# Block places given back in turn, a last output block done token tile by token tile, and W11 loaded once, in a one-core transformer block on Trainium2

## The chip, the core and the metric

The kernel runs on one core of a Trainium2 chip. The core has five engines with an instruction stream each: TensorE (PE; its weight loads are listed apart as PEld), VectorE (DVE), ScalarE (ACT), GpSimd (POOL) and SyncE (SP). Sixteen DMA engines move the data; loads are issued by SP, by ACT or, for loads that add onto what is there, by POOL. The metric is the time of one execution in microseconds (us): three runs of the kernel before gave 2258.97, 2261.0 and 2263.16, median 2261.0.

## What is computed

One block of a transformer in fp32, for one sequence of S = 512 tokens of width D = 2048, with a feed-forward width FF = 5632. The part that matters here is what follows the mixing of tokens:

```
sh_a, sc_a, g_a, sh_f, sc_f, g_f = split(silu(c) @ ada_w + ada_b, 6)      # "ada": six vectors of 2048
h = modulate(rms_norm(x, norm_mix), sh_a, sc_a);  proj = h @ w_in          # then convolutions and sparse attention
x = x + g_a * (concat(y_conv, y_attn) @ w_out)                             # out projection
h = modulate(rms_norm(x, norm_ffn), sh_f, sc_f)
x = x + g_f * ((silu(h @ ffn_w1) * (h @ ffn_w3)) @ ffn_w2)                 # FFN up, FFN down
```

## The kernel before

Each fp32 operand of a matmul is split in two parts, `hi` (rounded) and `lo` (the rest), and a product is lo·hi + hi·lo + hi·hi, three matmuls. A weight block is loaded by DMA, ACT casts it to `whi` (`w_hi`, L948) and DVE subtracts to get `wlo` (L953, L1262). The order in which each engine does its work is set by a scheduler from the program and its priorities; a tile's place is taken again only after the last reader of its former tile. SP issues its loads strictly in order: one that waits for a place holds all behind it.

The stages, in times of the profiled execution: input projection, compression and part of the ada vectors up to about 310 us; convolutions, attention and more ada up to 680; the out projection from 715 to 904; FFN up from 916 to 1791; FFN down from 1792 to 2257, and a short tail.

**Ada parts.** The FFN's shift, scale and gate are made by `ffn_parts`, a generator that is woven beside other work: one part is 16 loads of 256 KB and 16 instructions of DVE (L185). Parts 0 to 2 run beside `token_blocks` (up to 310 us), 3 to 9 beside the convolutions and the attention, the last two beside the last output block.

**Out projection to FFN up.** The output is made in four blocks of 512 columns (`token_block`, L98 to L100, three matmuls of 128x512 per token tile and 128 rows of weights). In a block, pairs of weight rows are the outer loop and the four token tiles the inner one, so the four tiles end together. Then, per tile, DVE multiplies by the gate and adds (L891, L892), and ACT takes the sum of squares (L893). After the fourth block follow the factor 1/rms of each token (L905 to L907, spread over partitions by the matmul L908), the transposes of the last block (`x2_turned(3)`, L871), the modulation of h (`modulated`, L985 on DVE and L986 on ACT, 128x512 for each of 16 k's), and `h_parts` (L976, L977), which splits h into the blocks `hC` that the products read.

**FFN up** is one level of Strassen: 44 units of 128 columns, for each of which seven products are formed from the blocks `hC[p]`, p = 1, 5, 6, 3, 7, 2, 4 (`product`, L960 and L962). The first two units (`PLAIN`) use four plain products from `hC[1..4]` while `h_sums` makes the rest. All `hC` lie in one pool, closed after the last unit.

**FFN down** is Strassen over four groups b of 5, 6, 6 and 5 units j, with seven products p per group in the order 1, 5, 6, 3, 7, 2, 4 (1, 2, 5, 6, 3, 7, 4 in group 0): 154 units of 12 matmuls 128x512 (L1282). The weights of a unit are four blocks W11, W12, W21, W22 of 512 KB, loaded by `w_load` a number of units ahead (`AHEAD`):

- p = 1: W11, into the ring `raw`
- p = 5: W11 again into a place of `t` (6 places), then W12 added onto it (L1237, POOL)
- p = 6: W22 into one of the 6 places `w`; DVE adds it to t (L1256). p = 3 uses W22 itself, so its place is free only after p3's split
- p = 7: W12 into a place of `w`, then W22 added (L1237, POOL)
- p = 2: W21 into a place of `w`; p = 4: W21 added onto t (L1251)

`a_parts` makes the other operand, `ghi`, `glo` and `e`, from gated rows `k0`, `k1` that `k_load` brings. `evict` adds finished products into y (L1301, L1303). `w_split` runs two units ahead of the matmuls.

Of the kernel before, what the change touches and what calls it, by code (L numbers as in the profile page):

```python
# [69 lines left out]
def block_kernel(ctx: ExitStack, tc: tile.TileContext, a: dict, out: bass.AP):  # L70
# [576 lines left out]
    early = ffn_parts(wring, 512, range(3))  # L647
    weave(beside(token_blocks(), early, 3.2), before_attention(), 1.5)
# [185 lines left out]
    later = ffn_parts(wring, 512, range(3, 10))  # L834
    weave(beside(convs(), later, 1.9), attention_steps(), 0.68)
# [19 lines left out]
    gd = [dram.tile([P, S], F32, name=f"gd{f}") for f in range(FF // P)]  # L855
    hst = ExitStack()
# [4 lines left out]
    xp = pool("x2", 2, stack=gst)  # L861
    tp = pool("tmp", 2, stack=gst)
    aring = pool("aring2", 3, stack=gst)
# [15 lines left out]
    for n in range(4):  # L879
        if n < 3:  # L880
            x_load(n + 1)
        ga = tp.tile([P, 512], F32, tag="ga", name="ga")
        ada_bcast(aux, ga, acc_g[-1])
        pst = [main() for _ in range(NT)]
        side = ada(aring, 1024, 2 * D + (n + 1) * 512, 512, acc_g, bias=True) if n < 3 else \
            ffn_parts(aring, 1024, (10, 11))
        weave(token_block(w_out, n * 512, yT, every[8:] + every[:8], pst), side, 1 if n < 3 else 2.5)
        for i, ps in enumerate(pst):
            t = tp.tile([P, 512], F32, tag="t", name="t")
            x2 = x2s[n][:, i, :]  # L890
            nc.vector.tensor_mul(t, ps, ga)  # L891
            nc.vector.tensor_add(x2, x2, t)  # L892
            nc.scalar.activation(t, x2, AF.Square, accum_out=ss2[:, i, n:n + 1])  # L893
        for i in range(0, NT, 2):
# [6 lines left out]
    rb = aux()  # L901
    for i in range(NT):
        dg = tp.tile([P, P], F32, tag="dg", name="dg")
        r2 = tp.tile([P, 1], F32, tag="r2", name="r2")
        nc.vector.reduce_sum(r2, ss2[:, i, :], axis=AX)  # L905
        rsqrt(r2, r2, D)
        nc.vector.tensor_scalar(dg, ident, r2, None, op0=ALU.mult)  # L907
        nc.tensor.matmul(rb[:, i * P:(i + 1) * P], ones, dg, start=True, stop=True)  # L908
# [11 lines left out]
    HS, HK = S // 2, KC // 2  # L920
    ust = ExitStack()
    dp = pool("up", 2)
    t2p = pool("t2", 1)
    hcp = pool("hC", 1, stack=ust)
    hC = {p: hcp.tile([P, HK, S], F32R, name=f"hC{p}") for p in (1, 5, 6, 3, 7, 2, 4)}
# [30 lines left out]
    def product(ps, wt, p, first, last):  # L956

        ks = [slice(k * P, (k + 1) * P) for k in range(HK)]
        for k in range(HK):
            nc.tensor.matmul(ps, wt[0][:, ks[k]], hC[p][:, k, :], start=first and k == 0, stop=False, skip_group_check=True)  # L960
        for k in range(HK):
            nc.tensor.matmul(ps[:, HS:], wt[1][:, ks[k]], hC[p][:, k, 0:HS], start=False, stop=last and k == HK - 1,  # L962
                             skip_group_check=True)
# [16 lines left out]

    def modulated(j, c, n, lower):

        for k in range(j * HK + c, j * HK + c + n):
            h = x2T[:, k, :]
            nc.vector.scalar_tensor_tensor(h, h, gsc[:, 1, k:k + 1], rb, op0=ALU.mult, op1=ALU.mult)  # L985
            nc.scalar.activation(h, h, AF.Identity, bias=shf[:, 1, k:k + 1])  # L986
        h_parts(1 + j, A[0, j][:, c:c + n, :], c, n)
        h_parts(lower, A[1, j][:, c:c + n, :], c, n)

    def h_sums(step):  # L990
# [4 lines left out]
        elif step == 1:  # L995
            nc.vector.tensor_sub(A[1, 1], A[1, 1], A[1, 0])
            h_parts(5, A[1, 1], 0, HK)
        elif step == 2:
# [15 lines left out]
    def plain_steps(u):  # L1014
# [3 lines left out]
        def make(q, w, j):  # L1018
# [3 lines left out]
            def mm(s):  # L1022
                if j == 0:
                    o[w] = [(main, aux)[w]() for _ in range(2)]
                for i, p in ((0, 1 + j), (1, (3, 4)[j])):
                    product(o[w][i], (s["hi"], s["lo"]), p, j == 0, j == 1)
# [15 lines left out]
        return [make(q, w, j) for q, w, j in ((11, 0, 0), (21, 0, 1), (12, 1, 0), (22, 1, 1))]  # L1042
# [67 lines left out]

    def k_load(b, half):
        n = GS[b]
        t = kraw[b, half] = krp.tile([P, GM, S], F32, tag=f"k{half}", name=f"k{half}")
        for j in range(n):
            nc.gpsimd.dma_start(t[:, j, :], gd[START[b] + half * n + j])
# [45 lines left out]
    modulated(0, 0, 2, 3)  # L1161
    modulated(0, 2, 2, 3)
    modulated(0, 4, 4, 3)
    for n, s in enumerate(order):
# [7 lines left out]
        if n < 4 * PLAIN:  # L1172
            h_sums(n)
        if n == len(order) - 5:
            zst.close()
            krp = pool("kraw", 1, side="right")
            for half in range(2):
                k_load(0, half)
        s["mm"](s)
        if n + 1 < len(order):  # L1180
            s["post"](s)
    ust.close()
# [5 lines left out]
    gpp = pool("gparts", 3)  # L1188
    tz = pool("tz", GM)
    wz = pool("wz", 6)  # L1190
    ep = pool("e", 1)
    yp = pool("y2", 3)
    yq = pool("y3", 1, side="right")
    y2 = [(yq if t == 3 else yp).tile([P, D], F32, tag="y", name="y") for t in range(NT)]
# [7 lines left out]
    def a_parts_(b, p):  # L1202
# [18 lines left out]
        hi = gpp.tile([P, GM, HS], F32R, tag="ghi", name="ghi")  # L1221
        lo = gpp.tile([P, GM, HS], F32R, tag="glo", name="glo")
# [4 lines left out]
    def w_load(b, p, j):  # L1227
# [5 lines left out]
        def get(pl, tag, one, plus=None):  # L1233
            t = pl.tile([P, HN], F32, tag=tag, name=tag)
            nc.sync.dma_start(t, one)
            if plus is not None:
                nc.gpsimd.dma_start(t, plus, accum_op=ALU.add)  # L1237
            return t

        if p == 1:  # L1240
            W[b, 11, j] = get(ring[0], "raw", block(0, 0))
        elif p == 5:
            W[b, "t", j] = get(tz, "t", block(0, 0), block(0, 1))
        elif p == 6:
            W[b, 22, j] = get(wz, "w", block(1, 1))
        elif p == 7:
            W[b, "t3", j] = get(wz, "w", block(0, 1), block(1, 1))
        elif p == 2:
            W[b, 21, j] = get(wz, "w", block(1, 0))
# [8 lines left out]
    def w_split(b, p, j):  # L1258
        t = W[b, {1: 11, 5: "t", 6: "t", 3: 22, 7: "t3", 2: 21, 4: "t"}[p], j]
# [76 lines left out]
    AHEAD = {1: 4, 5: 9, 6: 6, 7: 7, 2: 6, 4: 10}  # L1336

    def loads(n):
        for m in range(n + 13, n + 3, -1):
            if 0 <= m < len(units):  # L1340
                b, p, j = units[m]
                if (12 if (b, p) == (0, 5) else AHEAD.get(p)) == m - n:
                    w_load(b, p, j)

    for n in range(-13, 0):
        loads(n)
    for m in range(2):
        w_split(*units[m])
# [5 lines left out]
    for n, (b, p, j) in enumerate(units):  # L1354
# [16 lines left out]
        if n + 2 < len(units):  # L1371
            w_split(*units[n + 2])
# [35 lines left out]
```

## Time and profile before

| | before |
|---|---|
| median of three runs | 2261.0 us |
| profiled execution, its own time | 2263.49 us |
| its span (first to last instruction) | 2261.7 us |
| PE busy | 2182.5 us, 96% |
| DVE busy | 1725.9 us, 76% |
| ACT busy | 996.1 us, 44% |
| moved by DMA | 446.72 MB |

The time of a run is 1.8 us more than the span of its trace. Busy times are sums over instructions; matmuls are pipelined, so one shows 0.39 us while the next starts 0.23 us after it.

### The profile page before, as it was taken

The page shows a single profiled execution, that of the slowest core. Times are in us where ns is not written, and L with a number is a line of the kernel's source. Part 1 is how long each engine was busy: PE and PEld are TensorE (multiplying, and loading weights), DVE is VectorE, ACT ScalarE, POOL GpSimd, SP SyncE. Part 2 cuts the span into 40 slices and gives each one's busy share as a digit, 9 for nine tenths or more (in the row PEclk, how much of TensorE's full clock was granted, in tenths as well). Part 3 has the DMA queues.
Part 4 walks back from the last instruction along what each step waited for, and adds up shares of the span by engine and source line. Part 5 has one row for each costly group of instructions (what it writes and reads, how often), then busy time and mean ns, then how long its engine had stood idle before and what let it go on. Part 6 is the DMA issues. An engine that isn't in the chain of part 4 may idle for free.

```text
span 2261.7 us, 30554 instructions
## 1 busy us (share of the span) xinstructions
PE 2182.5 (96%) x11377; PEld 1812.0 (80%) x11377; DVE 1725.9 (76%) x2523; ACT 996.1 (44%) x1558; POOL 222.4 (10%) x267
## 2 busy tenths in 40 slices
PE   6999999999999999899999999999999998999998
PEld 5788778778777787788888888888888876777786
DVE  6878877877769755977878777887878776778697
ACT  5335235554444222744444444444444454444442
POOL 5310000000000000010000000000000121211111
PEclk9999999999999999999999999999999999999999
DMA  9965766544446865397776767677775699786966
GB/s 319 363 219 178 260 198 189 165 143 137 135 138 223 296 233 160 104 224 174 180 183 165 184 170 179 165 177 172 182 182 135 208 292 264 180 265 176 265 155 161
DMA packets 441096, 446.72 MB, mean 198 GB/s; under 512 B 18232, under 2 KB 345116, under 8 KB 440308
## 3 DMA queue, kind: packets, MB, share of 16 engines
q1 hardware_dynamic: 371764, 330.40, 46.7%
q0 software_dynamic: 69040, 114.12, 23.6%
q8 instruction: 89, 1.46, 0.3%
q14 instruction: 59, 0.48, 0.1%
q10 hardware_dynamic: 144, 0.26, 0.0%
HBM read 424.78 MB, written 19.93 MB: 197 GB/s over the span
## 4 chain that ended last, share of the span: by engine, by line
PE 73%; DMA 12%; DVE 11%; issue 2%; ACT 1%; POOL 0%; SPq 0%; DVEq 0%; ACTq 0%; POOLq 0%
PE main L960 14%; PE aux L960 10%; PE main L962 7%; PE main L98 6%; PE main L100 6%; PE main L99 6%; PE aux L1282 5%; PE aux L962 5%; DMA araw<-in_ada_w 5%; PE main L1282 5%; DMA w<-in_ffn_w 5%; DVE acc L185 2%; DVE wlo L1262 2%; PE aux L98 1%; DMA raw<-in_ffn_w 1%
## 5 line engine op out<-in xcount | busy, mean ns | idle before, releaser
L948 ACT CAST whi<-raw 128x1024 fp32r<-128x1024 f32 x282 | 295.3, 1047 | 351.5 <-PE main L960 114.0
L953 DVE TENSOR_TENSOR wlo<-raw,whi 128x1024 fp32r<-128x1024 f32 x260 | 315.4, 1218 | 81.2 <-ACT whi L948 80.8
L960 PE MATMUL main<-hC,whi 128*128 128x512 f32 x1408 | 356.7, 395 | 5.2 <-DVE hC L977 3.7
L960 PEld LDWEIGHTS main<-hC,whi 128*128 128x128 f32 x1408 | 255.1, 190 | 51.9 <-DVE hC L977 4.3
L960 PE MATMUL aux<-hC,whi 128*128 128x512 f32 x1072 | 270.1, 393 | 0.0
L185 DVE SCALAR_TENSOR_TENSOR acc<-araw,cT,acc 128x512 f32<-128x512 f32 x248 | 185.6, 748 | 73.2 <-DMA araw<-in_ada_w 60.2
L960 PEld LDWEIGHTS aux<-hC,whi 128*128 128x128 f32 x1072 | 193.7, 190 | 34.9
L962 PEld LDWEIGHTS main<-hC,wlo 128*128 128x128 f32 x1408 | 192.1, 190 | 13.8
L962 PE MATMUL main<-hC,wlo 128*128 128x256 f32 x1408 | 196.3, 282 | 0.0
L98 PE MATMUL main<-alo,whi 128*128 128x512 f32 x448 | 182.8, 408 | 1.4 <-DVE alo L347 1.4
L948 ACT CAST whi<-t 128x1024 fp32r<-128x1024 f32 x108 | 113.5, 1052 | 152.7 <-PE aux L1282 42.1
L99 PE MATMUL main<-ahi,wlo 128*128 128x512 f32 x448 | 176.6, 394 | 0.0
L100 PE MATMUL main<-ahi,whi 128*128 128x512 f32 x448 | 176.5, 395 | 0.0
L92 ACT CAST whi<-raw 128x1024 fp32r<-128x1024 f32 (+2 forms) x84 | 79.5, 949 | 207.0 <-PE main L100 138.6
L962 PEld LDWEIGHTS aux<-hC,wlo 128*128 128x128 f32 x1072 | 146.3, 190 | 12.4 <-DVE wlo L953 1.9
L98 PE MATMUL main<-wlo,ahi 128*128 128x512 f32 x384 | 152.9, 398 | 0.0
L99 PE MATMUL main<-whi,alo 128*128 128x512 f32 x384 | 151.8, 395 | 0.0
L962 PE MATMUL aux<-hC,wlo 128*128 128x256 f32 x1072 | 149.9, 282 | 1.5 <-DVE wlo L953 1.5
L100 PE MATMUL main<-whi,ahi 128*128 128x512 f32 x384 | 151.1, 394 | 0.0
L1262 DVE TENSOR_TENSOR wlo<-w,whi 128x1024 fp32r<-128x1024 f32 x66 | 79.9, 1222 | 81.3 <-ACT whi L948 81.2
L1282 PE MATMUL aux<-wlo,ghi 128*128 128x512 f32 x308 | 123.1, 400 | 16.2 <-DVE wlo L1262 16.2
L1049 DVE TENSOR_TENSOR raw<-raw 128x1024 f32<-128x1024 f32 x84 | 102.3, 1218 | 47.1 <-DMA raw<-in_ffn_w 47.0
(317 smaller groups left out, 4069.5 us busy)
## 6 DMA issues: line engine op xcount, KB each, us to landing
raw<-in_ffn_w SPq DMA_DIRECT2D x219, 512.0 KB, 4.9
araw<-in_ada_w SPq DMA_DIRECT2D x176, 256.0 KB, 3.0
w<-in_ffn_w SPq DMA_DIRECT2D x66, 512.0 KB, 8.0
t<-in_ffn_w POOLq DMA_DIRECT2D x65, 512.0 KB, 8.5
araw<-in_ada_w POOLq DMA_DIRECT2D x56, 512.0 KB, 14.4
raw<-in_w_in SPq DMA_DIRECT2D x128, 192.0 KB, 2.7
t<-in_ffn_w SPq DMA_DIRECT2D x43, 512.0 KB, 5.7
araw<-in_ada_w SPq DMA_DIRECT2D x40, 512.0 KB, 5.4
```

The source lines that it names most:

```text
L92: nc.scalar.copy(hi[:, :m], raw[:, :m])
L98: nc.tensor.matmul(ps, lhs[0], rhs[1], start=first, stop=False)
L99: nc.tensor.matmul(ps, lhs[1], rhs[0], start=False, stop=False)
L100: nc.tensor.matmul(ps, lhs[0], rhs[0], start=False, stop=last)
L185: nc.vector.scalar_tensor_tensor(acc, w, s, acc, op0=ALU.mult, op1=ALU.add)
L948: nc.scalar.copy(hi, t)
L953: nc.vector.tensor_sub(lo, t, hi.bitcast(F32))
L960: nc.tensor.matmul(ps, wt[0][:, ks[k]], hC[p][:, k, :], start=first and k == 0, stop=False, skip_group_check=True)
L962: nc.tensor.matmul(ps[:, HS:], wt[1][:, ks[k]], hC[p][:, k, 0:HS], start=False, stop=last and k == HK - 1, skip_group_check=True)
L1049: nc.vector.tensor_add(to, x, y)
L1262: W["last"] = nc.vector.tensor_sub(lo, t, hi.bitcast(F32)).ins
L1282: nc.tensor.matmul(ps[2 * t + c], x_[:, j, tok], w[:, cs], start=m == 0 and j == 0 and p in (1, 5, 2), stop=m == 2 and j == GS[b] - 1 and ...
```

## The change

Five things are done; the numbers in the code are those of the diff.

1. **Ada.** One of the early parts of `ffn_parts` is done in the later stage; both weaving rates follow.
2. **Last output block.** For the last four k's of block n = 3 both weight pairs are loaded, and the twelve matmuls of each token tile are done together, tile after tile; `normed(i)` then makes the tile's sum, squares and factor while the next tile's matmuls run.
3. **h by token groups.** The first half of K is modulated in halves of 256 tokens (`modulated_half`), and the products of unit 0 go chunk by chunk, with both weights.
4. **Places of hC.** Each block has a pool of its own and is given back after the last product that reads it; the places of the down phase (`kraw`, `tz`, `ghi`, `e`, `glo`, `wz`) take their room one by one.
5. **Weights of the down phase.** W11 is loaded once, into t, and split there for p1; W12 is added onto it right after that split. W22, W12 and W21 take ten places in turn, four of the ring `raw` and six `w`.

```diff
-    def token_block(w, c0, lhs, order, pst):
+    def token_block(w, c0, lhs, order, pst, each=None):
         for j in range(0, KC, 2):
+            if each and j == KC - 4:
+                wss = [load_split(ring, rows(w, order[jj], 2, c0, 512), 2, 512) for jj in (j, j + 2)]
+                for i in range(NT):
+                    tok = slice(i * P, (i + 1) * P)
+                    for k in range(4):
+                        mm3(pst[i], [h[:, tok] for h in lhs[order[j + k // 2 * 2] + k % 2]],
+                            [t[:, k % 2, :] for t in wss[k // 2]], False, k == 3)
+                    each(i)
+                    yield
+                return
...
-    early = ffn_parts(wring, 512, range(3))
-    weave(beside(token_blocks(), early, 3.2), before_attention(), 1.5)
+    early = ffn_parts(wring, 512, range(2))
+    weave(beside(token_blocks(), early, 3.5), before_attention(), 1.5)
...
-    later = ffn_parts(wring, 512, range(3, 10))
-    weave(beside(convs(), later, 1.9), attention_steps(), 0.68)
+    later = ffn_parts(wring, 512, range(2, 10))
+    weave(beside(convs(), later, 2.15), attention_steps(), 0.68)
...
+        def normed(i):
+            through(i)
+            if i % 2 == 0:
+                diag[i // 2] = accp.tile([P, S], F32, tag="acc", name="dg")
+            dg = diag[i // 2][:, i % 2 * P:(i % 2 + 1) * P]
+            r2 = tp.tile([P, 1], F32, tag="r2", name="r2")
+            nc.vector.reduce_sum(r2, ss2[:, i, :], axis=AX)
+            rsqrt(r2, r2, D)
+            nc.vector.tensor_scalar(dg, ident, r2, None, op0=ALU.mult)
+            if i == 1:
+                factor(0)
...
+            rb, diag = aux(), {}
+            weave(token_block(w_out, n * 512, yT, every[8:] + every[:8], pst, normed), side, 3.0)
...
+    def modulated_half(i, c, n, lower):
+        for k in range(c, c + n):
+            h = A[i, 0][:, k, :]
+            nc.vector.scalar_tensor_tensor(h, h, gsc[:, 1, k:k + 1], rb[:, i * HS:(i + 1) * HS], op0=ALU.mult,
+                                           op1=ALU.mult)
+            nc.scalar.activation(h, h, AF.Identity, bias=shf[:, 1, k:k + 1])
+        h_parts(lower if i else 1, A[i, 0][:, c:c + n, :], c, n)
...
+                if u == 0 and j == 0:
+                    for i in range(2 * w):
+                        if i:
+                            factor(1)
+                            for c in range(0, HK, 2):
+                                modulated_half(1, c, 2, 3)
+                        for k in range(HK):
+                            for v in range(2):
+                                product(o[v][i], (o["s", v]["hi"], o["s", v]["lo"]), (1, 3)[i], True, False, [k])
+                    return
...
+    def given_back(p):
+        hcst[p].close()
+        right = lambda *args: pool(*args, side="right")
+        if p == 1:
+            later["k"], later["t"] = right("kraw", 1), right("tz", GM)
+            for half in range(2):
+                k_load(0, half)
+        elif p in (5, 6, 3, 7):
+            name, n = {5: ("ghi", 3), 6: ("e", 1), 3: ("glo", 3), 7: ("wz", 6)}[p]
+            later[name] = right(name, n)
...
+        def place():
+            W["n"] = W.get("n", -1) + 1
+            pl, tag = (ring[0], "raw") if W["n"] % 10 < 4 else (wz, "w")
+            return pl.tile([P, HN], F32, tag=tag, name=tag)
...
         if p == 1:
-            W[b, 11, j] = get(ring[0], "raw", block(0, 0))
+            W[b, "t", j] = get(tz.tile([P, HN], F32, tag="t", name="t"), block(0, 0))
         elif p == 5:
-            W[b, "t", j] = get(tz, "t", block(0, 0), block(0, 1))
+            nc.gpsimd.dma_start(W[b, "t", j], block(0, 1), accum_op=ALU.add)
         elif p == 6:
-            W[b, 22, j] = get(wz, "w", block(1, 1))
+            W[b, 22, j] = get(place(), block(1, 1))
         elif p == 7:
-            W[b, "t3", j] = get(wz, "w", block(0, 1), block(1, 1))
+            t = W[b, "t3", j] = get(place(), block(0, 1))
+            nc.gpsimd.dma_start(t, block(1, 1), accum_op=ALU.add)
...
-    AHEAD = {1: 4, 5: 9, 6: 6, 7: 7, 2: 6, 4: 10}
+    AHEAD = {1: 5, 6: 9, 7: 12, 2: 9, 4: 15}
```

What the scheduler makes of it is seen in the order of instructions. TensorE at the end of the last output block, before (L908 spreads the factors, L871 are the transposes, L960 the first products of FFN up):

```order
L100 MATMUL main<-whi,ahi 128x512
L408 MATMUL aux<-acc,const 1x512
L908 MATMUL aux<-dg,const 128x128 x2
L871 MATMUL aux<-const,x_7437 128x128 x5
L908 MATMUL aux<-dg,const 128x128
L871 MATMUL aux<-const,x_7437 128x128
L908 MATMUL aux<-dg,const 128x128
L871 MATMUL aux<-const,x_7437 128x128 x10
L960 MATMUL main<-hC_8175,whi 128x512 x2
```

The same place now, from the second factor matmul inside the block (L915; the first stands ten rows further up) on; L890 are the transposes, L994 and L996 the products:

```order
L915 MATMUL aux<-dg,const 128x128
L100 MATMUL main<-whi,ahi 128x512
...
L99 MATMUL main<-whi,alo 128x512
L100 MATMUL main<-whi,ahi 128x512
L890 MATMUL aux<-const,x_7441 128x128 x12
L994 MATMUL main<-hC_6767,whi 128x512
L996 MATMUL main<-hC_6767,wlo 128x256
L994 MATMUL main<-hC_6767,whi 128x512
L996 MATMUL main<-hC_6767,wlo 128x256
L890 MATMUL aux<-const,x_7441 128x128 x4
```

The factors of tiles 0 and 1 have moved into the block, and the first products stand right behind twelve transposes; those of the second token half (L915 x2) follow seven rows below.

SyncE's loads in the down phase, before, from the end of group 0 on (raw is W11 for p1, t is W11 for p5, w is W22, W12 and W21):

```order
L1235 DMA w<-in_ffn_w 128x1024 x10
L1235 DMA t<-in_ffn_w 128x1024 x5
L1235 DMA raw<-in_ffn_w 128x1024 x6
L1235 DMA w<-in_ffn_w 128x1024 x18
L1235 DMA t<-in_ffn_w 128x1024 x6
L1235 DMA raw<-in_ffn_w 128x1024 x6
```

And now, from the first loads of group 1 to the W11 of group 2 (t is the one load of W11; raw and w are the ten places in turn):

```order
L1303 DMA w<-in_ffn_w 128x1024 x6
L1303 DMA raw<-in_ffn_w 128x1024 x4
L1303 DMA w<-in_ffn_w 128x1024
L1303 DMA t<-in_ffn_w 128x1024 x5
L1303 DMA w<-in_ffn_w 128x1024 x5
L1303 DMA raw<-in_ffn_w 128x1024 x4
L1303 DMA w<-in_ffn_w 128x1024 x6
L1303 DMA raw<-in_ffn_w 128x1024 x3
L1303 DMA t<-in_ffn_w 128x1024 x6
```

Of the 18 loads into places of a group, the first ten now stand ahead of the last five loads of its W11, and no W11 is loaded a second time.

GpSimd's adding loads of group 1, before (L1237 is W12 for p5 and W22 for p7, L1251 is W21 for p4, L1115 brings k):

```order
L1237 DMA t<-in_ffn_w 128x1024 x5
L1251 DMA t<-in_ffn_w 128x1024 x3
...
L1251 DMA t<-in_ffn_w 128x1024 x3
L1237 DMA w<-in_ffn_w 128x1024 x6
L1115 DMA k_17458<-gd_6748 128x512
```

And now (L1309 is W12 for p5, L1314 W22 for p7, L1318 W21 for p4):

```order
L1314 DMA raw<-in_ffn_w 128x1024 x3
L1314 DMA w<-in_ffn_w 128x1024
L1309 DMA t<-in_ffn_w 128x1024 x6
L1318 DMA t<-in_ffn_w 128x1024 x3
...
L1318 DMA t<-in_ffn_w 128x1024 x3
L1314 DMA w<-in_ffn_w 128x1024 x2
```

Four of the six sums for p7 are now issued ahead of all six for p5, where all six stood behind those for p4.

## Rows read from the trace of the kernel before

**Rows 1.** The page, first part: busy time, share of the span, instructions.

```profile
PE 2182.5 (96%) x11377; PEld 1812.0 (80%) x11377; DVE 1725.9 (76%) x2523; ACT 996.1 (44%) x1558; POOL 222.4 (10%) x267
```

**Rows 2.** List of waits, TensorE: releaser, us in total, times, longest us.

```profile
PE aux L1282 <- DVE wlo L1262: 16.2, 12, 3.7
PE main L1282 <- DVE wlo L1262: 14.7, 12, 4.7
```

**Rows 3.** Windows, line L1282 alone, of six products: span, busy (x), PEclk, DMA share, GB/s.

```profile
1807.00:1826.80 19.80, 15.69 (x61) 12.15 (x60) 0.91 1.04 322
1867.70:1891.70 24.00, 16.54 (x61) 12.49 (x61) 0.86 0.88 271
1969.40:1995.60 26.20, 20.88 (x86) 15.33 (x85) 1.00 1.05 309
...
2094.80:2120.70 25.90, 20.82 (x86) 15.28 (x85) 1.00 1.03 302
2208.70:2229.50 20.80, 15.84 (x62) 12.38 (x61) 0.92 0.96 240
...
2028.30:2046.10 17.80, 16.92 (x74) 13.37 (x73) 1.00 1.03 299
```

**Rows 4.** Chain that ended last, 1940 to 2030: start, us, what.

```profile
1966.58 11.44 DMA w<-in_ffn_w
...
1978.58 11.75 DMA w<-in_ffn_w
...
1995.82 16.32 PE main L1282 x72
```

**Rows 5.** Timeline of SyncE's queue, 1940 to 1996: start, us, loads.

```profile
1953.02 42.94 SPq L1235 DMA_DIRECT2D w<-in_ffn_w  x14
```

**Rows 6.** DMA of 1790 to 2230: queues (packets, MB, share), issues (median us to landing).

```profile
q0 software_dynamic: 12512, 44.57, 48.4%
q1 hardware_dynamic: 15557, 56.65, 35.0%
...
w<-in_ffn_w SPq DMA_DIRECT2D x66, 512.0 KB, 8.0
...
w<-in_ffn_w POOLq DMA_DIRECT2D x22, 512.0 KB, 11.0
```

**Rows 7.** Timeline of TensorE where FFN down begins.

```profile
1792.42 0.96 PE L1282 MATMUL main<-wlo,ghi 128*128 128x512 f32 x3 [1.65 <-ACT ghi L1223]
1793.95 0.50 PE L1282 MATMUL main<-whi,glo 128*128 128x512 f32 x1 [0.57 <-DVE glo L1224]
```

**Rows 8.** Timelines of TensorE and VectorE between out projection and FFN up.

```profile
904.06 0.39 PE L100 MATMUL main<-whi,ahi 128*128 128x512 f32 x1
...
916.54 2.08 PE L960 MATMUL main<-hC,whi 128*128 128x512 f32 x4 [3.75 <-DVE hC L977]
...
910.95 4.04 DVE L985 SCALAR_TENSOR_TENSOR x2T<-x2T,gsc,aux 128x512 f32<-128x512 f32 x6 [1.02 <-PE aux L908]
```

**Rows 9.** Groups by form of VectorE, 900 to 970, and a window of all engines.

```profile
L891 DVE TENSOR_TENSOR t<-main,ga 128x512 f32<-128x512 f32 x4 | 2.6, 687 | 0.2 <-ACT t L893 0.2
...
L971 DVE TENSOR_TENSOR d<-main,d 128x256 f32<-128x256 f32 x5 | 2.0, 417 | 0.1
...
917.00:943.60 26.60, 26.60 (x136) 22.70 (x136) 25.36 (x27) 23.70 (x30) 0.00 (x0) 0.89 0.14 41
```

**Rows 10.** Ada: its group on VectorE, and windows (PE, PEld, DVE, ACT, POOL busy).

```profile
L185 DVE SCALAR_TENSOR_TENSOR acc<-araw,cT,acc 128x512 f32<-128x512 f32 x248 | 185.6, 748 | 73.2 <-DMA araw<-in_ada_w 60.2
...
296.00:310.00 14.00, 11.04 (x42) 7.85 (x41) 8.28 (x21) 4.58 (x7) 0.00 (x0) 0.88 0.79 229
310.00:680.00 370.00, 366.60 (x1861) 294.21 (x1860) 280.02 (x591) 181.18 (x417) 2.10 (x4) 1.00 0.51 151
```

**Rows 11.** Timeline of VectorE in the last group's product 7.

```profile
2211.68 1.23 DVE L1262 TENSOR_TENSOR wlo<-w,whi 128x1024 fp32r<-128x1024 f32 x1 [3.74 <-ACT whi L948]
...
2218.42 2.35 DVE L1262 TENSOR_TENSOR wlo<-w,whi 128x1024 fp32r<-128x1024 f32 x2
```

More of the change, by code (lines that the diff above doesn't have):

```diff
@@ L855, in block_kernel, with block_place @@
     gd = [dram.tile([P, S], F32, name=f"gd{f}") for f in range(FF // P)]
+    HS, HK = S // 2, KC // 2
+    hC, hcst = {}, {p: ExitStack() for p in (1, 4, 2, 7, 3, 6, 5)}
+    def block_place(p, **kw):
+        hC[p] = pool(f"hC{p}", 1, stack=hcst[p], **kw).tile([P, HK, S], F32R, name=f"hC{p}")
+    block_place(1, side="right")
     hst = ExitStack()
@@ L899, in block_kernel @@
             x2_turned(n)
[L901 to L908, printed above, removed]
     x2_turned(3)
@@ L954, in w_lo, with product @@
         return lo
-    def product(ps, wt, p, first, last):
+    def product(ps, wt, p, first, last, chunks=range(HK)):
         ks = [slice(k * P, (k + 1) * P) for k in range(HK)]
-        for k in range(HK):
+        for k in chunks:
             nc.tensor.matmul(ps, wt[0][:, ks[k]], hC[p][:, k, :], start=first and k == 0, stop=False, skip_group_check=True)
-        for k in range(HK):
+        for k in chunks:
             nc.tensor.matmul(ps[:, HS:], wt[1][:, ks[k]], hC[p][:, k, 0:HS], start=False, stop=last and k == HK - 1,
@@ L1171, in block_kernel @@
         prepare(n + 2, "split")
-        if n < 4 * PLAIN:
+        if 0 < n < 4 * PLAIN:
             h_sums(n)
[L1174 to L1178, printed above, removed]
-        s["mm"](s)
+        s["mm"](s)
+        if s["u"] == NU - 1:
+            if s["p"] == 1:
+                zst.close()
+            given_back(s["p"])
+        if n == 1:
+            h_sums(0)
         if n + 1 < len(order):
             s["post"](s)
[L1182 to L1194, printed above, removed]
+    ghip, glop, tz, wz, ep, krp = (later[name] for name in ("ghi", "glo", "t", "wz", "e", "k"))
+    yp = pool("y2", NT)
+    y2 = [yp.tile([P, D], F32, tag="y", name="y") for t in range(NT)]
     W, A_, bank = {}, {}, {}
@@ L1220, in a_parts_ @@
             src = {5: e, 6: e, 3: e, 7: a21, 2: a12, 4: a22}[p]
-        hi = gpp.tile([P, GM, HS], F32R, tag="ghi", name="ghi")
-        lo = gpp.tile([P, GM, HS], F32R, tag="glo", name="glo")
+        hi = ghip.tile([P, GM, HS], F32R, tag="ghi", name="ghi")
+        lo = glop.tile([P, GM, HS], F32R, tag="glo", name="glo")
         A_["first"] = nc.scalar.copy(hi[:, :n], src).ins
@@ L1335, in block_kernel, with split @@
     units = [(b, p, j) for b, p in prods for j in range(GS[b])]
-    AHEAD = {1: 4, 5: 9, 6: 6, 7: 7, 2: 6, 4: 10}
+    AHEAD = {1: 5, 6: 9, 7: 12, 2: 9, 4: 15}
     def loads(n):
-        for m in range(n + 13, n + 3, -1):
+        for m in range(n + 16, n + 3, -1):
             if 0 <= m < len(units):
                 b, p, j = units[m]
-                if (12 if (b, p) == (0, 5) else AHEAD.get(p)) == m - n:
+                if (7 if (b, p) == (0, 2) else 14 if b == 0 and p == 4 else AHEAD.get(p)) == m - n:
                     w_load(b, p, j)
-    for n in range(-13, 0):
+    def split(n):
+        w_split(*units[n])
+        if units[n][1] == 1:
+            w_load(units[n][0], 5, units[n][2])
+    for n in range(-16, 0):
         loads(n)
     for m in range(2):
-        w_split(*units[m])
+        split(m)
     a_parts(*prods[0])
@@ L1371, in block_kernel @@
         if n + 2 < len(units):
-            w_split(*units[n + 2])
+            split(n + 2)
         if last and p == 4:
```

48 lines of the change are left out of this document (26 added, 22 removed).

## Prediction, made before the changed kernel had run

> **What bounds the kernel now.** I read the busy times first: TensorE works 96% of the span [rows 1], so only its idle and slow stretches can be won; the change removes no matmul. The list of waits then shows where it idles: the largest entry is L1282, FFN down, waiting for DVE's wlo, 24 waits of together 30.9 us [rows 2]. DVE is only the messenger, as the next views show.
>
> Product by product, L1282 alone says where in FFN down. A run of 72 matmuls that waits for nothing takes 16.32 us, 0.2267 us each [rows 4]. Against that, the four stretches of product 7 take 24.00 us for 61 matmuls, 26.20 for 86, 25.90 for 86 and 20.80 for 62, where 13.8, 19.5, 19.5 and 14.1 would do: 10.2 + 6.7 + 6.4 + 6.7 = 30.0 us lost (second to fifth row of [rows 3]). Product 2 of group 0 loses 19.80 - 61 x 0.2267 = 6.0 us (first row of [rows 3]), product 1 of group 2 17.80 - 74 x 0.2267 = 1.0 us (last row of [rows 3]). [...]
>
> The chain of waits tells why product 7 is late: it leads through a plain load into w (11.44 us) and then the load that adds onto it (11.75 us), back to back [rows 4]. Over the whole stage these land in 8.0 and 11.0 us at the median [rows 6]: 19 us for a pair that is issued at most 7 units (19 us) before its matmuls and is needed 2 units (5.4 us) earlier, for the split. SyncE's queue stands with 14 loads of w for 42.94 us [rows 5]: the six places hold W22 until product 3's split, so the pair cannot start earlier whatever `AHEAD` says. The sixteen DMA engines carry 48.4 + 35.0 = 83% meanwhile [rows 6], and 0.88 to 1.05 in the stalled stretches [rows 3]: near full, not full on the average.
>
> **The change part by part**, against the profiled execution's own 2263.5 us.
>
> *Places and lead in FFN down.* With ten places in turn, a load gets the place of the tenth load before it. For product 7 that is mostly a W21 long since split: all five pairs of groups 0 and 3 and four of the six of groups 1 and 2, which by the order now stand ahead of that group's p5 sums. The other two get a place of W22 when product 3's split frees it: 10 units, 27.2 us, before their own split, against 19 us for the pair. So all of product 7 should arrive in time: -30.0. What is late next is DVE. In the last group it worked without a gap from the wlo that ended at 2212.9 to the next at 2218.42 (sums into y and a `glo`) while TensorE waited for that wlo [rows 11]; some 3 us of this no load can cure: +3.0. Product 2 of group 0 had its places only as FFN up ended; now it uses the ring `raw`, free earlier: -6.0. Product 1 of group 2 gets W11 into t as soon as the last group's p4 split frees it, 6 units (16.3 us) before its split, against 8.0 us: -1.0. Stalls at product boundaries that the slack of product 7 used to absorb: DVE will have 30 us less to spread its work; I take +1.0, between 0 and the 3 us of the last group.
>
> *W11 once.* 22 loads of 512 KB, 11.5 MB of the stage's 44.57 + 56.65 MB, fall away. q1's share per MB is 35.0 / 56.65, so they are 7% of the engines' 440 us, 31 us of engine time that no instruction waits for as such. The price is a new chain: W12 can be added onto t only after p1's split, where a copy of W11 was there before. Groups 1 to 3 leave 5 or 6 units, 13.6 or 16.3 us, against 11.0 us; group 0 leaves 10 units. Hidden, with 2.6 us to spare: 0 (bounds 0 and +9, below).
>
> *Places of hC.* At the start of FFN down TensorE waits 1.65 us for `ghi` and 0.57 for `glo` [rows 7]; k0 now starts when hC1 falls free, six products before the end. Bounds 0 and -2.2; taken -1.5, since ACT still makes `ghi` among the casts of the last unit. W11 into t and the early W22 find room before the end too; that is in the -6.0.
>
> *Last output block and h by halves.* From the last L100 at 904.06 to the first product at 916.54 [rows 8] TensorE executes only transposes and factors. By the order the first product now stands 12 transposes behind the last L100, so up to 8 us could be won if that were all. But what follows is bound by those who make h: in the 26.6 us after the start DVE is busy 25.36 and ACT 23.70 [rows 9]. So I count DVE's time. Before, it began to modulate at 910.95, 6.9 us after the last L100 [rows 8]; now the sums and factors of tiles 0 to 2 lie under the matmuls of the block and only tile 3's are left, two passes of 0.687 us [rows 9] and the small ones: some 2.8 us, a gain of 4.1. Against it stand 11 more DVE instructions, since halves are 256 wide: a pass of 512 takes 0.687 and one of 256 0.417 [rows 9], so each split costs 2 x 0.417 - 0.687 = 0.147, together 1.6 us. -2.5, bounds -8 and +6 (if the pieces come in late one by one and the clock falls as in [rows 9], 0.89).
>
> [...]
>
> *Ada.* Around 300 us TensorE is busy 11.04 of 14 us at a DMA share of 0.79 [rows 10]: 3 us lost where a compression weight comes late among ada's loads. One part less takes 16 loads and 16 x 0.748 = 12 us of DVE out of this stage: -2.0 (bounds 0 and -3). They land between 310 and 680 us, where DVE is busy 280 of 370 us and DMA 0.51 [rows 10]: +0.5, at most the part's 12 us if that cover were gone.
>
> Sum: -30.0 + 3.0 - 6.0 - 1.0 + 1.0 - 1.5 - 2.5 - 2.0 + 0.5 = -38.5. On the own time 2225.0; the median of the three runs is 2.5 us lower than this execution, so **2222 us**.
>
> [...]
>
> **The rivals.**
>
> *A, as summed*, with a spread of its own: the hand-overs and small terms move it by 5 down or 9 up, 2217 to 2231.
>
> *B, the DMA engines stay the limit.* Less 31 us of engine time, the stage still carries 0.83 x 440 - 31 = 336 us in a stage that would be 403 us long, 83% again. For it: stalled stretches at 1.03 to 1.05 [rows 3], and an adding load that took 11.75 us [rows 4] will not land faster in the same crowd. Against: more places let loads use the quiet stretches. If half of the 34 us won from late weights (-30 + 3 - 6 - 1) stays lost: 2222 + 17 = 2239.
>
> *C, h by halves backfires.* More, smaller instructions on two engines that are 89 to 95% busy [rows 9], and TensorE fed by chunks at a low clock: +6 in place of -2.5, 2230.5. Against: the DVE sum above.
>
> *D, slower: W12 comes late for p5.* The one new chain, on t: p1's split, then the adding load, then p5's split, with 13.6 to 16.3 us. If the load took L, each of groups 1 to 3 would wait about L - 15 us once (its loads then follow one another at the same distance). At 18 us that costs 9 us, 2231; only at L = 15 + 43 / 3 = 29 us in all three groups would the whole gain be gone and the time be over 2265. The median of 11.0 [rows 6] speaks against, and so does the lighter load on the queue.
>
> *E, next to no change:* product 7 is late for another reason than its places, for instance DVE's own order as in [rows 11]. Without the 34 us the sum is -4.5, or 2256.5, and 2261 if the hand-overs give nothing. The chain through two loads [rows 4] speaks against.
>
> **How the numbers follow.** A 0.63, B 0.20, C 0.10, D as far as slower 0.03, E 0.04. The likeliest is A, 2222. The low end: the hand-overs and ada at their good ends (-8, -2.2 and -3 for -2.5, -1.5 and -2.0) make it 2215, and without DVE's 3 + 1 us and the +0.5 it is 2210; I go to 2208, for the waits that I have not counted. The high end, 2243, takes in C and B, with 4 us beyond the half that B takes. Left out are D, E, and a B that loses more. A measurement of this kernel can tell about 0.2%, 4.5 us, from no change: faster by more than that is A, B, C, 0.93; within it most of E, 0.03; slower 0.04.
>
> **What would show it.** In the changed kernel's trace, product 7 in each group should take 0.2267 us per matmul to within 3 us, and the waits of L1282 for wlo should fall from 30.9 us to under 8. SyncE's waits for wlo may stay long; they are cover then. The adding loads into raw and w should land before ACT's cast asks for them. The gap from the last output matmul to the first product should shrink to about 5 us, with new short waits of the products for hC behind it, and the last of unit 0 some 2.5 us nearer. Wrong it would be if L1282 waited instead for casts whose releaser is a DMA into t (D) or still one into w (B), if DVE in the two or three stretches after 916 us grew by more than 2 us (C), or if time appeared in 310 to 680 us (ada), which I have put at 0.5.

## The result: 2238.2 us, 1% faster, and the profile after

The changed kernel takes 2238.2 us at the median of four runs (2234.8 to 2241.0) against 2261.1 before; the ratio is 0.9898, 95% interval 0.9878 to 0.9918. The range of the prediction holds it, but the time lies 16 us above the likeliest, 2222, and close to the 2239 of rival B. The profile says that it got there in another way than B.

The page after, first part:

```profile
PE 2183.5 (98%) x11377; PEld 1808.0 (81%) x11377; DVE 1729.5 (77%) x2534; ACT 998.3 (45%) x1569; POOL 222.6 (10%) x267
```

The span fell from 2261.7 to 2238.7 us, TensorE's busy share rose from 96 to 98% [rows 1]. The list of waits of TensorE in the changed kernel (releaser, us, times, longest; L1349 is FFN down, was L1282):

```profile
PE aux L615 <- ACT late L612: 4.5, 1, 4.5
PE main L994 <- DVE hC L1011: 4.3, 2, 4.1
PE aux L996 <- DVE wlo L987: 3.6, 1, 3.6
...
PE aux L1349 <- DVE wlo L1329: 1.4, 2, 1.0
...
PE main L1349 <- DVE wlo L1329: 0.4, 1, 0.4
```

FFN down waited 30.9 us for wlo [rows 2]; now it waits 1.8. The windows of L1349 alone answer to [rows 3]: first all of group 0, then product 7 of the groups 0 to 3, product 2 of group 0 and product 1 of group 2 (span, TensorE busy, weight loads busy, clock, DMA share, GB/s):

```profile
1799.70:1898.00 98.30, 98.30 (x421) 78.76 (x422) 1.00 1.00 279
1869.80:1883.80 14.00, 14.00 (x61) 11.25 (x60) 1.00 0.84 251
1965.70:1982.50 16.80, 16.80 (x74) 13.50 (x73) 1.00 0.92 339
2084.00:2100.80 16.80, 16.80 (x74) 13.49 (x73) 1.00 0.90 319
2190.70:2206.00 15.30, 14.27 (x61) 11.17 (x60) 1.00 0.43 69
1813.80:1827.80 14.00, 14.00 (x61) 11.25 (x60) 1.00 1.04 327
2016.10:2032.90 16.80, 16.80 (x74) 13.49 (x73) 1.00 0.93 173
```

TensorE is busy through each of them but product 7 of the last group, where 1.0 us is left. So the DMA engines did not stay the limit: in group 0 their mean share is 1.00, and TensorE waits for nothing.

What the prediction did not have is in the chain of waits:

```profile
1949.05 16.80 PE main L1349 x72
1965.85 16.80 PE aux L1349 x72
```

72 matmuls that wait for nothing took 16.32 us before [rows 4], 0.2267 us each; now they take 16.80, 0.2333 each, from the first of FFN down to the last, at a granted clock of 1.00. Over the stage's 154 x 12 = 1848 matmuls that is 12.3 us.

The rest is seen by comparing moments. The timelines of TensorE after, at the end of the out projection and of FFN up:

```profile
907.53 0.39 PE L100 MATMUL main<-whi,ahi 128*128 128x512 f32 x1
...
911.19 0.48 PE L994 MATMUL main<-hC,whi 128*128 128x512 f32 x1
...
1790.04 2.11 PE L994 MATMUL main<-hC,whi 128*128 128x512 f32 x8 [1.40 <-DVE d L1005]
1796.81 2.09 PE L994 MATMUL main<-hC,whi 128*128 128x512 f32 x8 [0.92 <-DVE d L1001]
...
1799.69 0.86 PE L1349 MATMUL main<-wlo,ghi 128*128 128x512 f32 x3
```

and of SyncE's queue, the third store of a unit of FFN up, before and then after:

```profile
1000.89 0.39 SPq L1012 DMA_DIRECT2D gd<-d  x1
```

```profile
1006.05 0.39 SPq L1054 DMA_DIRECT2D gd<-d  x1
```

The last output matmul starts 3.5 us later than before (907.53 against 904.06 in [rows 8]), the first product of FFN up 5.35 us earlier (911.19 against 916.54), the third store 5.2 us later, the first matmul of FFN down 7.3 us later (1799.69 against 1792.42 in [rows 7]); the span ends 23.0 us earlier. So FFN down with the tail gave 30.3 us, which is 42.6 less 12.3 for the slower pace, and all before it cost 7.3.

Where FFN up lost its early start can be followed product by product. The products that began at 978.51 and 1001.30 us before begin at 981.52 and 1006.46 now: 3.0 us late, then 5.2. Between these two TensorE waits for a weight. Its load in the chain of waits and the wait in TensorE's timeline, before and then after:

```profile
987.08 9.26 DMA raw<-in_ffn_w
998.85 1.21 PE L962 MATMUL aux<-hC,wlo 128*128 128x256 f32 x8 [1.47 <-DVE wlo L953]
```

```profile
988.60 12.89 DMA raw<-in_ffn_w
1004.01 1.50 PE L996 MATMUL aux<-hC,wlo 128*128 128x256 f32 x8 [3.61 <-DVE wlo L987]
```

The DMA share from 985 to 1003 us is 1.03 before and 1.15 after. At 1014 us FFN up is 6.0 us late, and it stays within 0.3 us of that until 1780.

### The profile page after: what moved, and what is told of

It reads as the page before. It is cut to its first block, busy times and chain, and to the rows that moved or that the text cites. A ratio compares the mean times of both kernels' runs of the same rounds, so it can differ in the third digit from the quotient of the medians.

```text
span 2238.7 us, 30556 instructions
## 1 busy us (share of the span) xinstructions
PE 2183.5 (98%) x11377; PEld 1808.0 (81%) x11377; DVE 1729.5 (77%) x2534; ACT 998.3 (45%) x1569; POOL 222.6 (10%) x267
## 4 chain that ended last, share of the span: by engine, by line
PE 78%; DMA 11%; DVE 8%; issue 1%; ACT 1%; SPq 0%; POOL 0%; DVEq 0%; ACTq 0%; POOLq 0%
PE main L994 14%; PE aux L994 10%; PE aux L1349 8%; PE main L1349 8%; DMA araw<-in_ada_w 8%; PE main L996 7%; PE main L98 5%; PE main L100 5%; PE main L99 5%; PE aux L996 5%; PE aux L779 2%; DVE acc L185 1%; PE aux L751 1%; DMA raw<-in_ffn_w 1%; DVE wlo L1329 1%
## 5 line engine op out<-in xcount | busy, mean ns | idle before, releaser
L982 ACT CAST whi<-raw 128x1024 fp32r<-128x1024 f32 x288 | 301.5, 1047 | 350.9 <-PE main L994 111.6
L994 PE MATMUL main<-hC,whi 128*128 128x512 f32 x1408 | 360.4, 396 | 8.3 <-DVE hC L1011 4.3
L994 PEld LDWEIGHTS main<-hC,whi 128*128 128x128 f32 x1408 | 255.7, 191 | 56.5 <-DVE hC L1011 5.0
L994 PE MATMUL aux<-hC,whi 128*128 128x512 f32 x1072 | 272.2, 394 | 0.0
L994 PEld LDWEIGHTS aux<-hC,whi 128*128 128x128 f32 x1072 | 193.8, 190 | 34.7
L982 ACT CAST whi<-t 128x1024 fp32r<-128x1024 f32 x130 | 136.4, 1049 | 188.7 <-PE main L1349 60.9
L996 PEld LDWEIGHTS main<-hC,wlo 128*128 128x128 f32 x1408 | 194.0, 191 | 14.3
L996 PE MATMUL main<-hC,wlo 128*128 128x256 f32 x1408 | 199.2, 283 | 0.0
L100 PE MATMUL main<-ahi,whi 128*128 128x512 f32 x448 | 176.2, 394 | 0.0
L996 PEld LDWEIGHTS aux<-hC,wlo 128*128 128x128 f32 x1072 | 147.5, 191 | 14.3 <-DVE wlo L987 4.0
L996 PE MATMUL aux<-hC,wlo 128*128 128x256 f32 x1072 | 152.4, 283 | 3.6 <-DVE wlo L987 3.6
L100 PE MATMUL main<-whi,ahi 128*128 128x512 f32 x384 | 150.5, 392 | 0.0
L1329 DVE TENSOR_TENSOR wlo<-t,whi 128x1024 fp32r<-128x1024 f32 x88 | 106.3, 1223 | 27.2 <-ACT whi L982 26.7
L1349 PE MATMUL aux<-wlo,ghi 128*128 128x512 f32 x308 | 122.1, 396 | 1.6 <-DVE wlo L1329 1.4
```

The lines of the kernel that those rows point to most:

```text
L100: nc.tensor.matmul(ps, lhs[0], rhs[0], start=False, stop=last)
L982: nc.scalar.copy(hi, t)
L1329: W["last"] = nc.vector.tensor_sub(lo, t, hi.bitcast(F32)).ins
L1349: nc.tensor.matmul(ps[2 * t + c], x_[:, j, tok], w[:, cs], start=m == 0 and j == 0 and p in (1, 5, 2), stop=m == 2 and j == GS[b] - 1 and ...
```

## Experiments

Each kernel was compared with the kernel before on the same chip; its median lay between 2263 and 2267 us there, so the ratios are what can be compared. "Before" and "after" name the two kernels of the study. One traced execution of each gives these moments in us: the matmul that waits for the compression weight `late` (L604, now L615), the last output matmul, the first product of FFN up, the first matmul of FFN down, and how long FFN down takes with the tail.

| kernel | `late` | last output | FFN up | FFN down | FFN down and tail |
|---|---|---|---|---|---|
| before | 303.2 | 904.1 | 916.5 | 1792.4 | 469.3 |
| b_shift32 | 304.1 | 903.5 | 916.0 | 1793.9 | 471.7 |
| b_weights | 303.4 | 906.5 | 917.9 | 1797.7 | 433.2 |
| after | 308.4 | 907.5 | 911.2 | 1799.7 | 439.0 |
| a_again | 306.7 | 906.2 | 909.8 | 1797.6 | 439.1 |
| a_al2048 | 310.2 | 908.4 | 912.0 | 1800.0 | 429.6 |
| a_six | 307.2 | 906.3 | 910.0 | 1789.2 | 463.4 |
| a_ada | 303.5 | 904.5 | 908.2 | 1794.8 | 439.1 |
| a_whole | 308.6 | 909.0 | 919.6 | 1800.8 | 439.0 |
| a_block | 308.5 | 904.6 | 912.4 | 1794.0 | 439.0 |
| a_old_hand | 306.1 | 903.0 | 913.3 | 1791.7 | 439.0 |
| best2 | 302.7 | 899.8 | 910.1 | 1786.8 | 429.6 |

**The changed kernel again** (a_again).

> The changed kernel once more, as the measure for the three beside it. Both theories of the slower pace in FFN down: 233.3 ns from one matmul of L1349 to the next throughout the stage, in every execution, about 2238 us. If the pace were an accident of one execution, 226.7 ns here and about 2226 us.

2238.5 us, ratio 0.9887 (0.9868 to 0.9906). Its matmuls in FFN down stand 0.2333 us apart again: the pace belongs to the program, not to one execution.

**Where ghi and glo lie.** The operands that TensorE loads as weights in FFN down are `ghi` and `glo`; what streams past them is `whi` and `wlo`. By the programs' memory maps, which no trace prints, the places of these two are the same in all versions, 256 bytes past a multiple of 2048. In the kernel before, `ghi` and `glo` lie at such places too; the new pools put them on the other side of the memory, at 2016 past a multiple. Four kernels move them and nothing that TensorE reads besides (tiles of other engines behind them move along). a_aligned, in `given_back`:

```diff
+            if p == 5:
+                right("pad", 1).tile([P, 8], F32, name="pad")
             later[name] = right(name, n)
```

> The changed kernel with an unused tile of 32 bytes per partition ahead of ghi, so that ghi and glo, the stationary operands of FFN down, begin at multiples of 64 bytes, as in the kernel before, and not 32 bytes past one. Theory address: the pace of L1349 returns from 233.3 to 226.7 ns, 1848 x 6.6 ns = 12.3 us less, about 2226 us. Rival state (the pace is a state that the stage keeps as it begins, since nothing long interrupts it any more): nothing changes, 2238 us, 233.3 ns.

b_shift32, the kernel before:

```diff
+    pool("pad", 1).tile([P, 8], F32, name="pad")
     gpp = pool("gparts", 3)
+    pool("pad2", 1).tile([P, 8], F32, name="pad2")
```

> The kernel before with ghi and glo moved by 32 bytes, nothing else. Theory address: stretches without a wait go at 233.3 ns in place of 226.7; some of it hides in waits that exist anyway (product 7), so between 8 and 12 us more, about 2270 us. Rival state: 226.7 ns after each wait as before, 2261 us.

a_al128 and a_al2048 are a_aligned with `[P, 24]` and `[P, 440]`:

> The changed kernel with an unused tile of 96 bytes per partition ahead of ghi, so that ghi and glo begin at multiples of 128 bytes, as in the kernel before. With 32 bytes they began 64 past such a multiple, and the pace was 228.9 ns. Theory address, finer: the pace depends on the place within 128 bytes; 226.7 ns here, 1848 x 2.2 ns = 4 us less than with 32 bytes, about 2227 us. Rival (64 bytes is all that counts, and the rest of the difference to the kernel before has another cause): 228.9 ns and 2231 us.

> The changed kernel with an unused tile of 1760 bytes per partition ahead of ghi. It puts ghi and glo at 256 past a multiple of 2048 bytes, as in the kernel before, where the moving operands whi and wlo (256 past a multiple of 2048 too) lie in all versions. So far the pace was 226.7 ns at a distance of 0 between stationary and moving operand, modulo 2048, and 228.9 to 233.4 ns at 1664, 1728, 1760 and 288. Theory distance: 226.7 ns, 1848 x 6.6 ns = 12.3 us less than the changed kernel, about 2226 us. Rival (the side of the memory, or what lies beside ghi, counts): 229 to 234 ns, 2231 to 2238 us.

(288 in this text is the place of ghi in b_shift32; the distance there is 32.) One row each of their chains of waits, in the order b_shift32, a_aligned, a_al128, a_al2048:

```profile
1998.70 16.80 PE main L1284 x72
```

```profile
1962.12 16.48 PE aux L1351 x72
```

```profile
1965.09 16.80 PE aux L1351 x72
```

```profile
1962.45 16.32 PE aux L1351 x72
```

| kernel | place of ghi, glo modulo 2048 | distance to whi, wlo | per matmul | time | ratio (interval) |
|---|---|---|---|---|---|
| before | 256 | 0 | 226.7 ns | 2261.1 us | 1 |
| b_shift32 | 288 | 32 | 233.3 | 2267.5 | 1.0011 (0.9997 to 1.0025) |
| after | 2016 | 1760 | 233.3 | 2238.2 | 0.9898 (0.9878 to 0.9918) |
| a_aligned | 1984 | 1728 | 228.9 | 2231.4 | 0.9858 (0.9838 to 0.9879) |
| a_al128 | 1920 | 1664 | 233.3 | 2238.0 | 0.9881 (0.9860 to 0.9903) |
| a_al2048 | 256 | 0 | 226.7 | 2228.9 | 0.9848 (0.9827 to 0.9868) |

The rival, that the stage keeps whatever pace it begins with, fell with the first two: 32 bytes alone bring the matmuls of the kernel before to 233.3 ns and those of the changed one to 228.9. My finer theory of multiples of 128 fell with a_al128. At distance 0 the pace came back in full. Which property of the place counts, and by what the matmul loses the time, stays open: whi and wlo were never moved, and only five distances were tried. b_shift32 lost 2 us by median and not 8 to 12, within its interval nothing, and 2.4 us of FFN down in its trace: where loads came late, a slower matmul mostly shortened the wait (L1284 waits 21.8 us for wlo there, against 30.9).

a_al2048 should have won 12.3 us. FFN down takes 9.4 us less in its trace (439.0 to 429.6); the ratios give 9 to 11. Its waits of L1351 for wlo are 3.9 us in place of 1.8, which is 2.1 of the missing 2.9; that the faster matmuls leave DVE less time at the product boundaries is the likely reason, not a tested one.

**Places or lead** (a_six): all three kinds of block in w alone.

```diff
-            pl, tag = (ring[0], "raw") if W["n"] % 10 < 4 else (wz, "w")
+            pl, tag = wz, "w"
```

> The changed kernel with W22, W12 and W21 in the six places w alone, loads asked for as early as now. Theory places: product 7's pair again starts only when product 3's splits free places, and some 25 us of its waits return; 2260 us. Rival lead (the earlier request and the lighter queue do it): waits under 10 us, 2240 us.

2260.3 us, ratio 0.9987 (0.9975 to 1.0000). The waits in FFN down are back, and the chain leads through the same pair of loads as in [rows 4]:

```profile
PE main L1349 <- DVE wlo L1329: 10.6, 7, 4.6
PE aux L1349 <- DVE wlo L1329: 9.0, 7, 3.7
```

```profile
1957.80 10.64 DMA w<-in_ffn_w
...
1969.00 11.36 DMA w<-in_ffn_w
```

With 22 loads fewer and requests for product 7 made five units earlier, six places still give 19.6 us of waits. FFN down takes 24.4 us longer than in the changed kernel, so the four places more are worth that, and rival E, by which places do not matter, is out. What remains of the change in the stage is not nothing: b_shift32, at the same pace (72 matmuls take 16.80 us in both), takes 471.7 us against 463.4 here, so the lighter queue, the lead and what else the change does there are together worth some 8 us. That the time as a whole comes out only 22 us longer has a cause ahead of the stage: FFN down begins 10.5 us earlier than in the changed kernel, and in its trace the load that came late at 1000 us takes 9.61 us in place of 12.89, and the wait for it is 0.3 us in place of 3.6. The edit changes nothing there; why it is so stays open.

**Weights without the rest** (b_weights): the kernel before with part 5 alone (`place`, `w_load`, `AHEAD` and the adding load behind p1's split as in the change).

> The kernel before with part 5 alone: W11 once, ten places in turn, the new AHEAD; the places of hC are given back at the end of FFN up as before. Theory places: the waits of product 7 go here too, 30 us, and the pace stays 226.7 ns, since ghi and glo lie where they were; but W11 into t can only start when FFN up has ended, some 8 us for the load and 2 for the split, so the start of FFN down waits about 10 us; -30 - 1 + 10, about 2240 us. Rival (the start hides it, the ring is not needed): 2230 us or less.

2232.9 us, ratio 0.9868 (0.9849 to 0.9887): faster than the change as a whole by its median, though the intervals overlap. The start does pay:

```profile
1797.75 1.65 PE L1285 MATMUL main<-wlo,ghi 128*128 128x512 f32 x3 [3.99 <-DVE wlo L1265]
1800.63 0.77 PE L1285 MATMUL main<-whi,glo 128*128 128x512 f32 x1 [1.23 <-DVE glo L1224]
```

5.2 us in place of 2.2 [rows 7], where I had expected 10; but ghi and glo lie where they were, and 72 matmuls take 16.32 us. Giving the places back in turn (part 4) thus saved up to 5 us at the start of FFN down and cost 12.3 by the places that it chose.

**Hand-over from out projection to FFN up.** a_whole undoes part 3, a_block part 2, a_old_hand both; the cores of the edits, part 2 first and then part 3, shortened:

```diff
-            weave(token_block(w_out, n * 512, yT, every[8:] + every[:8], pst, normed), side, 3.0)
+            weave(token_block(w_out, n * 512, yT, every[8:] + every[:8], pst), side, 2.5)
+            for i in range(NT):
+                normed(i)
...
-    for c, n in ((0, 1), (1, 1), (2, 2), (4, 2), (6, 2)):
-        modulated_half(0, c, n, 3)
+    factor(1)
+    modulated(0, 0, 2, 3)
+    modulated(0, 2, 2, 3)
+    modulated(0, 4, 4, 3)
```

> The changed kernel with h made for all 512 tokens at once as before (part 3 undone; the last block is still done tile by tile, with factors made inside it). My forecast of the hand-over: halves cost 11 instructions of DVE, 1.6 us, and let products start early; without them DVE would be done sooner but the first product some 4 us later; the first units end within 2 us of the changed kernel. Rival C (halves backfire): 4 to 6 us less, about 2233 us.

> The changed kernel with the last output block done as before, pairs of weights outside and tiles inside, and factors after it; h is still made by halves. Undoing the halves alone gave 1.6 us more, undoing block and halves together 3.5 us less than the changed kernel. If the two parts add up, undoing the block alone gives 5 us less, about 2233 us. If the block's early factors are what the halves live on, it gives as much as the changed kernel or more, 2238 us.

> The changed kernel with the whole hand-over from out projection to FFN up as before (parts 2 and 3 undone). My forecast: 2.5 us more, about 2241 us. Rival, by the trace of the changed kernel, where the first units of FFN up stand 2.6 us further behind the kernel before than the last output matmul does: 2 to 4 us less, about 2235.5 us.

a_whole 2240.1 us, ratio 0.9890 (0.9872 to 0.9909); a_block 2237.0, 0.9893 (0.9874 to 0.9912); a_old_hand 2234.8, 0.9867 (0.9846 to 0.9888). Neither part by itself can be told from the changed kernel, and both together only by their medians, 3.5 us to the good of the old way; a_block missed the 2233 that adding up would give. So the hand-over did not give its 2.5 us; that it costs 3 is likely, not shown. The traces point the same way: from the matmul of `late` to the first of FFN down it is 1489.8 to 1492.2 us with the new block (after, a_again, a_al2048, a_ada, a_whole), 1484.1 to 1485.6 with the old one (a_block, a_old_hand, best2). The wait for a weight at about 1000 us is 3.6 to 4.2 us in those five and 0 to 1.7 in those three. But a_six, with the new block, has 1482.0 and 0.3. Where the early start went is shown by the window that answers to the last of [rows 9], in the changed kernel:

```profile
917.00:943.60 26.60, 22.25 (x108) 18.50 (x107) 24.18 (x29) 21.06 (x32) 0.00 (x0) 0.87 0.26 67
```

TensorE is busy 22.25 of the 26.6 us where it was busy throughout, at a mean clock of 0.87 (0.89 before); DVE is busy 24.18 us and ACT 21.06, against 25.36 and 23.70. The products begin earlier and then stand waiting for hC, 4.1 us in one piece.

**Ada as before** (a_ada): `range(3)` at 3.2 and `range(3, 10)` at 1.9 again.

> The changed kernel with the ada parts divided as before (three early, at rate 3.2, the rest at 1.9). As predicted, one part less in the early stage should have saved 2 us there and cost 0.5 later; so undoing it would cost 1.5, about 2240. What the trace of the changed kernel shows, out projection matmuls 1.5 us later at 800 us than before, says the opposite: undoing it gains 1 to 2 us, about 2236.5.

2235.1 us, ratio 0.9869 (0.9846 to 0.9892), 3.4 us less by medians, intervals overlapping. The window 242 to 317 us (PE, PEld, DVE, ACT, POOL busy, clock, DMA share), before, after and a_ada:

```profile
242.00:317.00 75.00, 71.42 (x371) 51.23 (x370) 52.78 (x119) 18.24 (x40) 0.62 (x2) 0.98 0.76 248
```

```profile
242.00:317.00 75.00, 67.13 (x347) 47.70 (x347) 46.17 (x105) 17.44 (x39) 0.62 (x2) 0.98 0.73 233
```

```profile
242.00:317.00 75.00, 70.17 (x352) 49.87 (x351) 50.01 (x113) 17.72 (x40) 0.38 (x2) 0.93 0.74 242
```

The early stage did not get shorter: TensorE is busy 3 to 4 us less in this window with two parts than with three, and the matmul that waits for `late` comes later. It starts at 302.7 to 304.1 us in all five traces with three early parts and at 306.1 to 310.2 in the others; before, after and a_ada:

```profile
L604 PE MATMUL aux<-const,late x2: 273/300/328, 303.2 to 303.4; 128*128 128x128 f32 x2
```

```profile
L615 PE MATMUL aux<-const,late x2: 421/449/477, 308.4 to 308.7; 128*128 128x128 f32 x2
```

```profile
L615 PE MATMUL aux<-const,late x2: 421/448/476, 303.5 to 303.7; 128*128 128x128 f32 x2
```

Whether the number of parts or the rate of 3.5 does it was not tried apart.

**What the experiments point to** (best2): 1760 bytes ahead of ghi, old hand-over, old ada, the rest as changed.

> Together: the changed kernel with the 1760 bytes ahead of ghi (9.5 us less by itself), the hand-over from out projection to FFN up as before (3.5 us less) and the ada parts divided as before (3.4 us less). The places in turn, W11 once and the blocks given back in turn stay. If the three add up, 2238.3 - 16.4 = 2222 us and a pace of 226.7 ns; if the earlier end of FFN up only meets loads of FFN down that are not there yet, 2228 us.

2223.0 us, ratio 0.9814 (0.9796 to 0.9833), below both kernels. By medians the three add up within 1 us; its five runs lie between 2218 and 2228. In its trace 72 matmuls take 16.32 us, and FFN down waits

```profile
PE aux L1343 <- DVE wlo L1323: 3.0, 3, 1.4
PE main L1343 <- DVE wlo L1323: 0.9, 1, 0.9
```

## Why the prediction was right, and where its steps failed

| step | predicted | measured in the traces |
|---|---|---|
| waits within FFN down | -30.0 + 3.0 - 6.0 - 1.0 + 1.0 = -33.0 | -42.6 |
| pace of the matmuls there | 0 | +12.3 |
| all before its first matmul (ada, last block, h by halves, its start) | -1.5 - 2.5 - 1.5 = -5.5 | +7.3 |
| sum | -38.5 | -23.0 |

The time lies in the range, but by luck in part. The waits came out 9.6 us better than summed, the pace 12.3 and the stages ahead 12.8 worse; what is left of these is the 15.5 us by which the sum missed. The measured 2238 lies outside the 2217 to 2231 that A was given for itself, and the upper end of the range, 2243, stood for B and C, neither of which came.

*Places of the loads: right.* Product 7 and the two smaller products run through, the last group keeps 1.0 us where I had left 3; a_six shows that the places do it. The term was 9.6 us too small: the stretches that I counted lose their waits and the half-clock matmuls behind these almost to nothing (after the wait of 4.70 us in product 7 of group 0 the kernel before has a granted clock of 0.50 from 1882 to 1888 us, with matmuls 0.43 us apart that last 0.63; in the changed kernel no matmul of the stage lasts longer than 0.50), and the small waits at other product boundaries, which I expected to grow by 1, shrank with them. The slower pace had a part in that: at 226.7 ns 3.9 us of waits stay (a_al2048), at 233.3 ns 1.8. Without it the waits gave 469.3 - 429.6 = 39.7 us.

*W11 once: right that it is hidden.* The 1.8 us of waits leave no room for rival D's 9. How much of a_six's 8 us comes from the loads removed was not tried by itself.

*Rival B: its number, not its mechanism.* The DMA share is 1.00 in the first 100 us of FFN down while TensorE never stops. A reader of the time alone would have taken B for shown. The share stood near 1 while the waits went, so it could not tell B from A.

*Places of hC: the step that failed.* I priced when the places come free and never asked where the new tiles would lie, so the pace of FFN down's matmuls was put at no change without a reason. They were taken as -1.5; the start gave 2.2, and two of FFN up's last products took 2.3 back (1.40 and 0.92, waits for d; the second of these evictions stands behind the first split of FFN down on DVE). Against it stand 12.3 us for the pace, the largest single miss.

*Hand-over: wrong in sign by the medians.* The first product came 3.7 us after the last L100, as the order said (about 5 predicted, 12.5 before). But I counted DVE's time as if its work could be done without gaps, and left out two things. The block itself got longer: from the matmul of `late` to the last L100 it is 599.1 us, and 596.9 with the old block (a_old_hand); that the last L100 starts 3.5 us later than in the kernel before is less than the 5.2 us that the ada stage lost. And behind the first products wait the next weights: by 980 us the lead of 5.35 us was a lag of 3.0, and the load that came late at 1000 us made 6.0 of it. Rival C's mark, DVE over 2 us more in the stretches behind 916 us, did not appear, and a_whole, which makes h as before, gained nothing; the price was paid by TensorE, standing between chunks.

*Ada: wrong.* I took the late weight to be behind the number of ada loads and counted -2.0; its matmul came 5.2 us later instead (3.2 between a_ada and a_again). The wait itself tells little: 3.0 us before and 4.5 after, but 3.8 in a_again, 3.8 in a_ada and 4.1 in b_shift32, which has its ada parts as before.

One thing came as a gift that no term had: at 762 us the kernel before and b_weights wait 2.8 us for x before the transposes of the first output block (L871), the changed kernel 0.2. best2, which keeps only parts 4 and 5, does not wait there, so it comes with the pools of part 4, by which the places of x2 and of the ada ring moved; which of the two does it was not tried.

## What to carry to other kernels

When a pool moves, write down where the operands of TensorE come to lie and compare the pace of a run of matmuls without waits before and after: here 32 bytes moved it by 2 to 3% (226.7 to 233.3 ns, and 233.3 to 228.9), and it cost half a per cent of the kernel (12.3 of 2238 us). When a load is waited for, find the reader that holds its place: here four places more were worth 24 us where asking earlier left most of the waits. Starting a consumer early bought nothing here while its producers, and then the loads, were the bound (FFN up began 5.35 us earlier and was 6.0 us late at 1014 us): count the end of the producers' work, what the consumer does in the gaps, and what it will wait for next.

## What the runs showed of the hardware

The pace of the back-to-back matmuls of 128x512 in FFN down changed with the place of the operand that is loaded as weights: 226.7, 228.9 or 233.3 ns at a granted clock of 1.00, with that operand moved by 32 to 1760 bytes. The weight loads beside them last 187 to 188 ns at the median at 226.7 and at 233.3. No run here shows by what the running matmul loses the 2.2 or 6.6 ns. What the rows do show is that the matmul beside the load is slower when, of all that TensorE reads, the place of the weights alone is changed. A new place of an operand that streams in FFN up (hC1, by the memory map at 32 past a multiple of 64 in the changed kernel) made no such difference: FFN up's later units keep their distance to the kernel before within 0.3 us from 1014 to 1780 us.
